# A graph attention layer on one core: narrower row levels in the first sort, and the second sort on keys without their offset taken off

## The chip, the cores and the metric

The kernel runs on one core of a Trainium2 chip. The metric is the device time of one execution in microseconds (us). In the profile lines TensorE is "PE" (its weight loads "PEld"), VectorE "DVE", ScalarE "ACT", GpSimd "POOL" and SyncE, which here only issues transfers, "SP"; L201 is a line of the kernel.

## The reference

```python
for h in range(n_heads):                       # 4 heads, 4096 nodes, 64 features
    x_proj[h] = x @ weight[h]
# a score for each of 50,000 edges (leaky relu of a source part plus a target part)
for h in range(n_heads):
    for i in range(num_edges):
        output[h, dst[i]] += np.exp(edge_scores[h, i]) * x_proj[h, src[i]]
# ... and each target's sum is divided by the sum of its exp(scores) + 1e-8
```

## The kernel before

Each of the 128 partitions holds 391 edges as fp32 keys in a row of 512; the rest of the row is padding with the largest key. A bitonic sort orders each row (levels k = 1 to 9) and then merges the rows of every 8 partitions into 16 runs. The key is ordered by the source's group (16 of them), then target, then source within the group. The runs go to DRAM, each group of 8 partitions fetches its own source group's windows back, a second sort merges them, and a second fetch gives windows by target. These are unpacked into indices for a loop over 33 blocks of 125 targets, which gathers with one-hot matmuls and sums with further matmuls.

A step of the sort is a minimum and a maximum over the first `width` columns:

```python
def half(self, j, width=L):
    s, d = self.step()                         # source and destination alternate
    h = 1 << j
    n = width >> (j + 1)
    for o, op in ((0, OP.min), (h, OP.max)):
        V.tensor_tensor(out=av(d[:], o, [2 * h, n], [1, h]), in0=av(s[:], 0, [2 * h, n], [1, h]),
                        in1=av(s[:], h, [2 * h, n], [1, h]), op=op)

def rows(self, first, n=L):
    w8 = -(-n // 8) * 8                        # 392 for the first sort, 512 for the second
    w128 = n // 128 * 128 if n % 128 <= 8 else L   # 384 and 512
    for k in range(first, 10):
        w = w8 if k <= 3 else w128 if k <= 7 else L
        self.flip(k, w)
        for j in range(k - 2, -1, -1):
            self.half(j, w)
        # ... (an assertion on which buffer is current)
```

The second sort takes the group's offset off the fetched keys first, and ScalarE counts how many keys lie below each of 33 bounds while VectorE sorts. The unpacking adds the block's offset from a per-partition column:

```python
def group(pool, pp, start):
    raw = pool.tile([P, L], F32, name="raw")
    fetch(pool, skey1, start, W1, raw, 1)
    kr = pool.tile([P, L], F32, name="kr")
    V.tensor_scalar(out=kr[:], in0=raw[:], scalar1=goff[:, 0:1], scalar2=None, op0=OP.add)
    sgn = below(pool, kr[:], L, nb2, ND, 8 * NI)     # 33 Sign activations with sums
    so = Sorter(pool, kr)
    so.rows(9)
    store(skey2, so.runs())
    bounds(pool, pp, sgn, 8 * NI, L, [sel2[:]], off2, m8, 8, ws2, we2)
# ...
# in unpack(i): kb = win[:, i] + boff[:, i], then a shift and a mask of kb, then a cast
```

## Time and profile before

| | before |
|---|---|
| median of the first runs | 305.47 us (304.89 to 305.67) |
| first sort's keys stored, at | 70.73 us |
| second sort's keys landed, at | 78.51 us |
| first unpacking, at | 122.43 us |
| first one-hot of the loop, at | 127.41 us |
| last result, at | 295.48 us |

Two lines of the page of the kernel before: busy time and share of the span by engine, and the clock granted to TensorE in 40 equal slices, in tenths of full speed:

```profile
PE 203.1 (67%) x3534; PEld 192.0 (64%) x3534; DVE 267.4 (89%) x494; ACT 179.7 (60%) x352; POOL 26.1 (9%) x71
...
PEclk9999965555555555798999999999999999999998
```

No engine is full over the span, yet there are stages in which one is. The table by stretch, in the prediction below, shows them.

### The profile page before, as it was taken

The numbers are of one execution on the slowest core, as the hardware profiler recorded it, in microseconds if no ns is written. First come the engines' busy times: TensorE is split into PE (matmuls) and PEld (weight loads), VectorE is DVE, ScalarE is ACT, GpSimd is POOL, SyncE is SP. The second block draws the span as 40 slices with busy tenths as digits, with TensorE's granted clock in tenths as the row PEclk, the third lists the DMA queues.
The fourth block names the chain that finished last, engine by engine and source line by source line (L and its number), as shares of the span: only waits on it lengthen the run. The fifth ranks groups of instructions, "written<-read, shape, count | busy, mean of one in ns | idle before, by whom it ended". The sixth has DMA issues, their size and how long they took to land. (4 is left out here: it accounts for less than half of the span.)

```text
span 301.8 us, 8411 instructions
## 1 busy us (share of the span) xinstructions
PE 203.1 (67%) x3534; PEld 192.0 (64%) x3534; DVE 267.4 (89%) x494; ACT 179.7 (60%) x352; POOL 26.1 (9%) x71
## 2 busy tenths in 40 slices
PE   0002999940000000849999999999999999999990
PEld 0001699930000000349999999999999999999980
DVE  3999999996599997699999999999999999999970
ACT  2951700050499920337877877787777877787750
POOL 7880000001100001500000000000000000000000
PEclk9999965555555555798999999999999999999998
DMA  3035000000100000397486568766785578755012
GB/s 106 0 66 93 0 2 0 0 0 36 36 0 0 0 0 35 104 384 291 150 287 226 190 251 297 251 198 232 277 289 202 211 252 301 259 205 195 17 38 58
DMA packets 13070, 41.80 MB, mean 138 GB/s; under 512 B 3088, under 2 KB 8272, under 8 KB 8928
## 3 DMA queue, kind: packets, MB, share of 16 engines
q1 hardware_dynamic: 10632, 38.97, 36.5%
q10 hardware_dynamic: 1688, 1.55, 2.2%
q0 software_dynamic: 704, 0.66, 1.0%
q8 instruction: 30, 0.49, 0.7%
q14 instruction: 16, 0.13, 0.1%
HBM read 36.13 MB, written 5.05 MB: 136 GB/s over the span
## 5 line engine op out<-in xcount | busy, mean ns | idle before, releaser
L464 ACT CAST xs<-ps 128x1200 bf16<-128x1200 f32 (+1 forms) x98 | 102.7, 1048 | 0.0
L477 DVE TENSOR_TENSOR val<-xs,wv 128x4096 bf16<-128x4096 bf16 (+1 forms) x34 | 75.7, 2229 | 4.6 <-ACT xs L464 1.0
L456 PE MATMUL ps<-xa,oh 128*128 128x72 bf16 x528 | 72.5, 197 | 3.6 <-DVE oh L438 2.9
L460 PE MATMUL ps<-adb,oh 128*128 128x136 bf16 x528 | 73.5, 226 | 0.0
L458 PE MATMUL ps<-xa,oh 128*128 128x72 bf16 x528 | 71.7, 198 | 0.6 <-DVE oh L439 0.5
L496 PE MATMUL acc<-xs,val 128*128 128x125 bf16 x1056 | 63.7, 218 | 1.2
L496 PEld LDWEIGHTS <-val 128*128 128x128 bf16 x1056 | 59.1, 98 | 3.5 <-DVE val L477 3.5
L456 PEld LDWEIGHTS <-oh 128*128 128x128 bf16 x528 | 52.4, 100 | 3.5 <-DVE oh L438 3.5
L458 PEld LDWEIGHTS <-oh 128*128 128x128 bf16 x528 | 52.1, 99 | 2.0 <-DVE oh L439 1.4
L460 PEld LDWEIGHTS <-oh 128*128 128x128 bf16 x528 | 52.2, 99 | 0.0
L462 ACT ACTIVATE ex<-ps 128x96 bf16<-128x96 f32 (+1 forms) x99 | 25.0, 253 | 30.1 <-PE ps L460 30.1
L438 DVE TENSOR_SCALAR oh<-bc,pF 128x4096 bf16<-128x4096 bf16 (+2 forms) x35 | 42.7, 1219 | 0.1
L201 DVE TENSOR_TENSOR sA<-sB 128x256 f32<-128x256 f32 (+2 forms) x108 | 39.6, 408 | 1.8
L201 DVE TENSOR_TENSOR sB<-sA 128x256 f32<-128x256 f32 (+2 forms) x100 | 36.8, 409 | 1.7
L263 ACT ACTIVATE junk<-kr,nb 128x512 f32<-128x512 f32 x33 | 23.8, 722 | 13.6 <-DVE kr L314 12.5
L274 PE MATMUL cnt_ps<-sgn,sel 128*128 128x17 f32 (+1 forms) x6 | 1.7, 390 | 43.9 <-ACT sgn L266 43.9
L274 PEld LDWEIGHTS cnt_ps<-sgn,sel 128*128 128x128 f32 x6 | 1.4, 318 | 44.0 <-issue 44.0
L358 PEld LDWEIGHTS at_ps<-uv,xT 64*128 64x128 f32 x130 | 25.4, 303 | 0.2 <-issue 0.2
L358 PE MATMUL at_ps<-uv,xT 64*128 64x4 f32 x130 | 25.5, 332 | 0.0
L439 DVE TENSOR_SCALAR oh<-bc,pF 128x2048 bf16<-128x2048 bf16 (+2 forms) x35 | 25.1, 717 | 0.0
L542 PE MATMUL pf<-Wbd,aT 128*125 128x128 f32 x132 | 21.9, 288 | 0.9 <-ACT aT L538 0.9
L341 PE MATMUL ps<-ident,wS 64*128 64x64 f32 x2 | 0.7, 350 | 27.7 <-DMA wS<-in_weight_dram 27.7
(126 smaller groups left out, 219.3 us busy)
## 6 DMA issues: line engine op xcount, KB each, us to landing
bc<-gat_bins SPq DMA_DIRECT2D x32, 1024.0 KB, 9.0
out_dram<-res SPq DMA_DIRECT2D x32, 125.0 KB
gat_sorted<-sA SPq DMA_DIRECT2D x2, 256.0 KB
eS<-in_edge_index_dram SPq DMA_DIRECT2D x1, 390.0 KB
eD<-in_edge_index_dram ACTq DMA_DIRECT2D x1, 390.0 KB
gat_bins<-tb SPq DMA_DIRECT2D x9, 32.0 KB
out_dram<-res SPq DMA_DIRECT2D x1, 96.0 KB
win<-gat_sorted,wi POOLq DMA_INDIRECT x5, 2.6
```

Source lines behind the costliest of these rows:

```text
L201: V.tensor_tensor(out=av(d[:], o, [2 * h, n], [1, h]), in0=av(s[:], 0, [2 * h, n], [1, h]), in1=av(s[:], h, [2 * h, n], [1, h]), op=op)
L263: S.activation(out=junk[:], in_=v, func=ACTF.Sign, bias=nbnd[:, b:b + 1], scale=1.0, accum_out=sgn[:, b:b + 1])
L358: T.matmul(out=ps[:, b, :], lhsT=xT[:, b * step:b * step + P], rhs=uv[:, k, :], start=(b == 0), stop=True, skip_group_check=True)
L438: V.tensor_scalar(out=oh[:, 0:2, e], in0=bc[:, :, e], scalar1=pF[:, 0:1], scalar2=None, op0=OP.is_equal)
L439: V.tensor_scalar(out=oh[:, 2, e], in0=bc[:, 1, e], scalar1=pF[:, 1:2], scalar2=None, op0=OP.is_equal)
L456: T.matmul(out=ps[:, i, P:P + XC], lhsT=oh[:, 1, e], rhs=xa[:, 2 * t, :], start=(i % 2 == 0), stop=False, skip_group_check=True)
L458: T.matmul(out=ps[:, i, P:P + XC], lhsT=oh[:, 2, e], rhs=xa[:, 2 * t + 1, :], start=False, stop=False, skip_group_check=True)
L460: T.matmul(out=ps[:, i, 0:S0], lhsT=oh[:, 0, e], rhs=adb[:, b, :], start=False, stop=True, skip_group_check=True)
L462: S.activation(out=av(ex[:], 2 * t0, [2, n], [2 * NT, 2 * H], [1, 2]), in_=av(ps[:], P, [PW, n], [1, 2 * H], [0, 2]), func=ACTF.Exp)
L464: copy(out=xs[:, t0:t0 + n, 0:P + XC], in_=ps[:, 0:n, 0:P + XC])
L477: V.tensor_tensor(out=av(val[:], h * Dout, [Dout, n], [C, NT], [1, Din]), in0=av(xs[:], S0, [0, n], [XW, NT], [1, Din]), in1=av(wv[:], h * ...
L496: T.matmul(out=self.acc[:, k * BD:(k + 1) * BD], lhsT=val[:, t, k * P:(k + 1) * P], rhs=xs[:, t, 0:BD], start=False, stop=(t == NT - 1), s ...
```

## The change

The intent is to take work off VectorE where it works alone. The steps of levels 8 and 9 skip columns that hold padding only. The second sort compares the keys as they were fetched, since all keys of a run share one offset and their order does not depend on it; ScalarE takes the offset off for its counts, and the unpacking's column carries it for the rest. GpSimd prepares that column in the setup.

```diff
     boff = cst.tile([P, NI], F32)
+    pg = cst.tile([P, 1], F32)
+    G.tensor_scalar(out=pg[:], in0=pm16[:], scalar1=-float(SG * N), scalar2=None, op0=OP.mult)
     for i in range(NI):
         G.tensor_scalar(out=boff[:, i:i + 1], in0=p16[:], ...)
+        G.tensor_tensor(out=boff[:, i:i + 1], in0=boff[:, i:i + 1], in1=pg[:], op=OP.add)
@@ rows
                 for j in range(k - 2, -1, -1):
-                    self.half(j, w)
+                    self.half(j, w if k <= 7 or j > 6 else w128 if j > 2 else w8)
@@ group
-        V.tensor_scalar(out=kr[:], in0=raw[:], scalar1=goff[:, 0:1], scalar2=None, op0=OP.add)
+        S.activation(out=kr[:], in_=raw[:], func=ACTF.Identity, bias=goff[:, 0:1])
         sgn = below(pool, kr[:], L, nb2, ND, 8 * NI)
-        so = Sorter(pool, kr)
+        so = Sorter(pool, raw)
```

## The prediction

> **What bounds the kernel now.** I first read the table of busy time by stretch, cutting the span where the timelines of the engines show a change of work. VectorE is "DVE", ScalarE "ACT", GpSimd "POOL", TensorE "PE".
>
> ```profile
> core 0: us, PE busy (x) PEld busy (x) DVE busy (x) ACT busy (x) POOL busy (x), PEclk, DMA share, GB/s
> 5.70:26.40 20.70, 0.00 (x0) 0.00 (x0) 19.60 (x61) 13.35 (x35) 14.89 (x34) 1.00 0.29 58
> 26.40:39.80 13.40, 10.79 (x63) 8.11 (x63) 12.86 (x34) 6.93 (x13) 0.00 (x0) 1.00 0.00 0
> 39.80:70.60 30.80, 23.70 (x112) 23.57 (x111) 29.46 (x74) 4.50 (x5) 0.00 (x0) 0.50 0.00 1
> ...
> 78.50:116.90 38.40, 0.62 (x2) 0.50 (x2) 36.74 (x92) 27.08 (x67) 0.00 (x0) 0.50 0.00 0
> ...
> 200.00:240.00 40.00, 39.68 (x846) 38.82 (x843) 38.69 (x41) 31.35 (x58) 0.00 (x0) 1.00 0.68 241
> ```
>
> The kernel is three stages in a row. From 5.7 to about 70.6 us VectorE alone runs the first sort; its tenth of idle time is the few hundredths between dependent instructions. From 78.5 to 116.9 it runs the second sort. After about 123 us a loop over 33 blocks keeps PE busy 39.68 of 40 us and DVE 38.69. The share for the whole span (DVE 89%, PE 67%) hides this: before 123 us only DVE's own chain counts, and both parts of the change lie there. The chain that ended last is no help, since it reaches back only to 284.8 us.
>
> Next, the timeline of VectorE in the first sort, where a row is start, length, engine, line, operation, output, input and count. The rows differ in their width only:
>
> ```profile
> 9.03 0.64 DVE L201 TENSOR_TENSOR sA<-sB 128x196 f32<-128x196 f32 x2
> 9.70 0.36 DVE L191 TENSOR_TENSOR sB<-sA 128x196 f32<-128x196 f32 x1
> ...
> 24.37 0.63 DVE L201 TENSOR_TENSOR sB<-sA 128x192 f32<-128x192 f32 x2
> 25.04 0.63 DVE L201 TENSOR_TENSOR sA<-sB 128x192 f32<-128x192 f32 x2
> ...
> 33.51 0.76 DVE L201 TENSOR_TENSOR sB<-sA 128x256 f32<-128x256 f32 x2
> 34.31 0.76 DVE L201 TENSOR_TENSOR sA<-sB 128x256 f32<-128x256 f32 x2
> ```
>
> A step (one min, one max) starts every 0.67 us at 196 columns a half, 0.66 at 192, and 0.795 at 256 (34.31 to 35.10 gives 0.79, eight steps in a row average 0.795). Start to start is what counts on a chain, not the length of one. The level k = 8 begins at 26.36 and is the first at full width.
>
> Last, the head and the end of the second sort, on VectorE and then on ScalarE:
>
> ```profile
> 78.51 0.49 DVE L314 TENSOR_SCALAR kr<-raw,goff 128x512 f32<-128x512 f32 x1 [5.08 <-DMA raw<-gat_sorted,wi]
> 79.03 0.43 DVE L191 TENSOR_TENSOR sA<-kr 128x256 f32<-128x256 f32 x1
> ...
> 116.94 0.19 DVE L276 TENSOR_SCALAR cnt<-cnt_ps 128x41 f32<-128x41 f32 x1
> ```
>
> ```profile
> 79.17 0.72 ACT L263 ACTIVATE junk<-kr,nb 128x512 f32<-128x512 f32 x1 [12.54 <-DVE kr L314]
> ...
> 107.11 0.20 ACT L266 COPY sgn<-sgn 128x7 f32<-128x7 f32 x1
> ```
>
> The fetched keys land, VectorE subtracts the group's offset (it waited 5.08 us for the transfer), and only then do the sort and ScalarE's 33 counts start. The counts end at 107.31, and their result is first wanted at 116.94.
>
> [...] I found one table load in the trace, 1.28 us at 5.68, in front of the first Sign[...]. [...] Here the six steps from 7.68 to 11.71, beside POOL's setup, took 4.03 us, 0.672 each, against 0.668 worked out from the quiet 192-column steps[...]; no loss to speak of.
>
> **The change part by part.**
>
> Row levels. In k = 8 the halves j = 6 to 3 go from 512 columns to 384 and j = 2 to 0 to 392; in k = 9 the same, while its j = 7 and both flips stay full. With 391 edges a row, columns 392 to 511 hold only the padding maximum, so the skipped comparisons change nothing. Steps per level: four at 384 and three at 392, two levels: 8 x (0.795 - 0.660) = 1.08 us and 6 x (0.795 - 0.668) = 0.76 us, together 1.84 us. All of it is on VectorE's chain. The second sort has 512 real columns, so its widths stay.
>
> Offset of the second sort. The subtraction leaves VectorE: 79.03 - 78.51 = 0.52 us from the chain, since the first flip now waits for the transfer itself. In its place ScalarE runs one Identity of 512 elements, about 0.72 us (what a Sign of this shape takes in the row above), ahead of the counts. Its first Sign came 0.66 us after the keys landed; now it comes after 0.72 us and a hand-over that I put at 0.17 (kr ended at 79.00, Sign began at 79.17), 0.23 us later. Counts then end 107.31 - 78.51 + 0.23 = 29.0 us after landing, and VectorE wants them 116.94 - 78.51 - 0.52 = 37.9 us after. About 0.6 us of matmul between leaves 8 us of slack. Nothing is lost there.
>
> Unpacking. The offset goes into boff, a per-partition column that the unpacking already adds. Those five VectorE instructions (about 0.29 us each) stay as they are.
>
> Setup on POOL. One more tensor_scalar and five tensor_tensor on one column. The existing five boff instructions took 1.64 us, 0.33 each, so six take about 2.0 us. POOL's later transfers go out 2 us later. Its att vectors are issued by 19.3 and land 2.2 us later, near 21.5; moved to 23.5 they still precede PE's use at 28.36, which comes after weights that land at 27.68. boff itself is used at 122.4. Hidden.
>
> Sum: 1.84 + 0.52 = 2.36 us off a chain that sets the start of the loop. The store, second fetch and loop follow by data, and loop blocks repeat at a fixed rhythm, so all of it should reach the end: 305.47 - 2.36 = 303.11 us. The before median lies high in what was seen (304.89 to 305.67, and 304.22 for the profiled execution), so I put **303.0**.
>
> **The rivals.** (1) *TensorE's clock eats or adds to the gain.* [...] The trace has such a half-clock stretch at the loop's start, 135.4 to 138.7 (0.50 in those windows, 1.00 just before). If that were lost time, it is worth half of 3.3, 1.65 us, at most[...]. For it: PE is nearly full from there on. Against: the runs before spread over only 0.8 us. Times 301.4 to 304.8, the ends unlikely. (2) *ScalarE's counts become the bound of the second sort*, gaining nothing from the 0.52 and leaving 303.6. The 8 us of slack speaks against. (3) *A wait moves in.* The store's landing and the indirect fetch could hide part of the gain, if they were tied to something else; but both fetches follow VectorE's last instructions (the store goes out at 70.73, right at the end of the sort), so they move along. [...] (4) *Narrow steps save less*, if the fixed part of an instruction were all that mattered: refuted by the 0.66 against 0.795 above.
>
> **Range and chances.** The mechanism is arithmetic on durations of the same instructions; what is unsure is the clock's phase (about 0.7 us as I weigh it) and the median of few runs (0.4). Together some 0.8 either way: 302.1 to 304.0. Two per cent would be 6.1 us, more than twice the whole sum, so faster by over 2% gets 0.01, slower 0.01, same 0.98.
>
> **What would show it.** In the changed trace the fourteen steps should read 0.66 or 0.67 us start to start and the first sort's store go out near 68.9 in place of 70.73. The first flip of the second sort should start as the transfer lands, with an Identity on ScalarE beside it, no table load, counts ending about 29 us after landing and the sort about 37.9 after. The first unpacking should start near 120.1 instead of 122.43, and the blocks of the loop keep their rhythm. I am wrong if a new wait stands before the first flip, if VectorE's steps beside POOL's setup slow down, or if the half-clock stretch grows or goes and the loop's length with it.

The 0.668 us of a step at 196 columns is an estimate from the two widths in the trace: 64 columns are 0.795 - 0.660 = 0.135 us a step, so 4 more than 192 are 0.008. That the Identity would bring no table load was the assumption. The clock's phase in the range means when the half-clock stretch comes; the 0.7 us for it is an estimate out of the 1.65, and that the stretch could come otherwise was not shown by then (c1 shows it later: 10.2 us in place of 3.4).

## More of the kernel before

Lines of the changed kernel are numbered three higher from the middle on, and an experiment's may be a few more.

## The result

The changed kernel is correct and takes 302.82 us (median of 4 runs, 302.28 to 303.03) against 305.18 us (4 runs, 304.57 to 305.67). The ratio is 0.9921, with a 95% interval of 0.9897 to 0.9945. A ratio is the mean time of one kernel's fast runs over the mean of the other's in the same rounds, so it is not quite the ratio of the medians. The medians differ by 2.36 us.

The table by stretch of the changed kernel, cut where the same work begins and ends (columns as in the prediction):

```profile
core 0: us, PE busy (x) PEld busy (x) DVE busy (x) ACT busy (x) POOL busy (x), PEclk, DMA share, GB/s
5.64:26.34 20.70, 0.00 (x0) 0.00 (x0) 19.60 (x60) 13.34 (x35) 16.48 (x40) 1.00 0.27 57
26.34:38.07 11.73, 8.14 (x37) 5.57 (x38) 11.13 (x36) 6.20 (x12) 0.00 (x0) 1.00 0.01 3
38.07:68.83 30.76, 26.13 (x137) 25.63 (x134) 29.46 (x74) 5.28 (x7) 0.00 (x0) 0.56 0.00 1
76.68:114.62 37.94, 0.62 (x2) 0.50 (x2) 36.32 (x91) 27.80 (x68) 0.00 (x0) 0.50 0.00 0
200.00:240.00 40.00, 39.69 (x833) 38.83 (x831) 38.69 (x42) 31.74 (x59) 0.00 (x0) 1.00 0.70 246
```

Levels 8 and 9 are the second row: 11.73 us, where they took 13.52 (26.36 to the shuffle at 39.88). The levels beside GpSimd's setup, the first row, are as long as before (20.70 us) although GpSimd works 1.6 us more in it (16.48 us in place of 14.89). The merging, 30.76 us, took 30.74. The second sort, from the landing of its keys to the use of the counts, takes 37.94 in place of 38.43. The loop's own rates are the same.

The timeline of VectorE in level 8 of the changed kernel; the row at 29.78 starts 0.66 us after the one before it and is followed by one at 30.45:

```profile
28.46 0.63 DVE L204 TENSOR_TENSOR sB<-sA 128x192 f32<-128x192 f32 x2
29.12 0.63 DVE L204 TENSOR_TENSOR sA<-sB 128x192 f32<-128x192 f32 x2
29.78 0.64 DVE L204 TENSOR_TENSOR sB<-sA 128x196 f32<-128x196 f32 x2
```

The head of the second sort, VectorE first, then ScalarE:

```profile
76.68 0.43 DVE L194 TENSOR_TENSOR sA<-raw 128x256 f32<-128x256 f32 x1 [5.06 <-DMA raw<-gat_sorted,wi]
...
114.62 0.20 DVE L279 TENSOR_SCALAR cnt<-cnt_ps 128x41 f32<-128x41 f32 x1
```

```profile
77.11 0.72 ACT L317 ACTIVATE kr<-raw,goff 128x512 f32<-128x512 f32 x1 [9.79 <-DMA raw<-gat_sorted,wi]
77.87 0.72 ACT L266 ACTIVATE junk<-kr,nb 128x512 f32<-128x512 f32 x1
```

The first comparison itself now waits for the transfer, and ScalarE's Identity and counts run beside the sort. The counts end at 106.0 us, far ahead of 114.62. No table load stands before the Identity: the only one in the trace is at 5.64 us (1.28 us), in front of the first Sign, as before.

The first unpacking on VectorE, in the kernel before and then in the changed one:

```profile
122.43 0.29 DVE L379 TENSOR_SCALAR kb<-win,boff 128x128 int32<-128x128 f32 x1 [2.02 <-DMA win<-gat_sorted,wi]
```

```profile
120.14 0.29 DVE L382 TENSOR_SCALAR kb<-win,boff 128x128 int32<-128x128 f32 x1 [2.04 <-DMA win<-gat_sorted,wi]
```

One thing moved that nobody asked to move. TensorE's first work, on the weights, in the changed kernel:

```profile
28.60 0.34 PE L344 MATMUL ps<-ident,wS 64*128 64x64 f32 x1 [28.60 <-DMA wS<-in_weight_dram]
```

It began at 27.68 before. The eight small transfers of the att vectors, issued 2 us later by GpSimd, landed 2.1 to 7.6 us after their issue, where they had taken 2.1 to 2.7. The tables ended at 63.2 us in place of 62.5, which VectorE did not feel, since it asks for the result at 68.83.

### The profile page after: what moved, and what is told of

Read it like the earlier page. It is cut to its first block, busy times and chain, and to the rows that moved or that the text cites. A ratio compares the mean times of both kernels' runs of the same rounds, so it can differ in the third digit from the quotient of the medians.

```text
span 300.1 us, 8417 instructions
## 1 busy us (share of the span) xinstructions
PE 203.3 (68%) x3534; PEld 191.8 (64%) x3534; DVE 265.2 (88%) x493; ACT 180.4 (60%) x353; POOL 27.6 (9%) x77
## 5 line engine op out<-in xcount | busy, mean ns | idle before, releaser
L204 DVE TENSOR_TENSOR sA<-sB 128x256 f32<-128x256 f32 (+2 forms) x108 | 38.8, 400 | 1.9
L204 DVE TENSOR_TENSOR sB<-sA 128x256 f32<-128x256 f32 (+2 forms) x100 | 35.9, 400 | 1.7
L361 PEld LDWEIGHTS at_ps<-uv,xT 64*128 64x128 f32 x130 | 24.7, 296 | 0.4 <-issue 0.4
L361 PE MATMUL at_ps<-uv,xT 64*128 64x4 f32 x130 | 24.8, 327 | 0.0
```

Source lines behind the costliest of these rows:

```text
L361: T.matmul(out=ps[:, b, :], lhsT=xT[:, b * step:b * step + P], rhs=uv[:, k, :], start=(b == 0), stop=True, skip_group_check=True)
```

## The experiments

Where each run stands at the same points of the program, in us of its profile; the times are medians of the kernel and of the kernel before on the same chip.

| run | store | keys landed | counts used | first unpacking | first one-hot | last result | time | before |
|---|---|---|---|---|---|---|---|---|
| before | 70.73 | 78.51 | 116.94 | 122.43 | 127.41 | 295.48 | 305.18 | |
| changed | 68.94 | 76.68 | 114.62 | 120.14 | 125.58 | 293.51 | 302.82 | 305.18 |
| a1_rows_only | 68.85 | 76.64 | 115.09 | 120.59 | 126.07 | 294.12 | 302.45 | 304.13 |
| a2_offset_only | 70.83 | 78.58 | 116.51 | 122.11 | 127.14 | 295.08 | 303.68 | 304.13 |
| a3_all_wide | 74.49 | 82.20 | 120.65 | 126.19 | 131.59 | 299.52 | 308.28 | 304.13 |
| a4_after_again | 68.98 | 76.66 | 114.60 | 120.15 | 124.98 | 293.15 | 301.86 | 304.13 |
| b1_counts_late8 | 68.92 | 77.03 | 114.91 | 120.46 | 125.85 | 294.43 | 302.95 | 304.50 |
| b2_counts_late24 | 68.84 | 76.86 | 124.66 | 128.95 | 135.66 | 304.32 | 312.43 | 304.50 |
| b3_pool_late40 | 68.93 | 78.61 | 116.49 | 122.02 | 126.91 | 295.06 | 303.34 | 304.50 |
| b4_clock_held | 68.86 | 76.58 | 114.46 | 119.99 | 124.90 | 292.29 | 301.46 | 304.50 |
| c1_after_ref | 68.92 | 76.72 | 114.66 | 120.20 | 125.13 | 294.41 | 302.08 | 304.71 |
| c2_warm_early | 69.12 | 76.80 | 114.72 | 120.25 | 125.16 | 293.64 | 302.37 | 304.71 |
| c3_both_clock | 69.10 | 76.63 | 114.56 | 120.10 | 124.97 | 293.00 | 301.58 | 304.71 |
| c4_unpack_spread | 68.94 | 76.69 | 114.62 | 120.17 | 124.63 | 294.83 | 303.22 | 304.71 |

All results were correct. The theory is that VectorE's chain sets when the loop starts and the rest follows. Its rivals are the clock of TensorE, the counts on ScalarE, and a wait that moves in.

**Each part alone.** a1 is the kernel before with this edit, and a2 the kernel before with all the other edits of the change:

```diff
-                    self.half(j, w)
+                    self.half(j, w if k <= 7 or j > 6 else w128 if j > 2 else w8)
```

> The kernel before with the narrow row levels alone. My theory (VectorE's chain sets the start of the loop): the first sort's store goes out near 68.9 us instead of 70.73, the first unpacking starts near 120.6 instead of 122.43, and the time falls by 1.84 us. Rival 1[...]: unpacking as above, but the end of the span moves by less or more than 1.84 by up to 1 us. Rival 3 (a wait hides it): the store moves, the unpacking does not.

> The kernel before with the offset's move alone. Theory: store unmoved near 70.7, the first unpacking near 121.9 (0.52 us earlier), the time 0.5 us lower, which lies near the noise of a run, so the trace decides. Rival 2 (ScalarE's counts bind): the unpacking stays at 122.4.

VectorE's timeline in a1, then in a2:

```profile
76.64 0.49 DVE L314 TENSOR_SCALAR kr<-raw,goff 128x512 f32<-128x512 f32 x1 [5.10 <-DMA raw<-gat_sorted,wi]
...
120.59 0.28 DVE L379 TENSOR_SCALAR kb<-win,boff 128x128 int32<-128x128 f32 x1 [2.02 <-DMA win<-gat_sorted,wi]
```

```profile
78.58 0.42 DVE L194 TENSOR_TENSOR sA<-raw 128x256 f32<-128x256 f32 x1 [5.06 <-DMA raw<-gat_sorted,wi]
...
122.11 0.29 DVE L382 TENSOR_SCALAR kb<-win,boff 128x128 int32<-128x128 f32 x1 [2.11 <-DMA win<-gat_sorted,wi]
```

In a1 the landing moves by 1.87 us and the unpacking by 1.84. In a2 nothing moves before the landing, and from the landing to the use of the counts it takes 116.51 - 78.58 = 37.93 us against 38.43: 0.50 us. The unpacking shows only 0.32 of it, since this execution was already 0.07 late at the landing and the window came another 0.11 later. By time, a1 is 0.995 (0.9928 to 0.9971) of before and a2 0.9989 (0.997 to 1.0008). The second interval holds 1: the total time cannot show half a microsecond, but the trace can. A wait that hides the gain is out.

**All levels wide.** The same lever the other way:

```diff
-            w8 = -(-n // 8) * 8
-            w128 = n // 128 * 128 if n % 128 <= 8 else L
+            w8 = w128 = L
```

> The kernel before with no row level narrowed at all: all 512 columns in levels 1 to 9. This is the same lever pushed the other way, to see the size per step and whether the end follows one to one. 22 steps go from 192 to 256 columns a half (0.135 us each) and 6 from 196 to 256 (0.127), flips among them 4 and 3, which makes 26 steps of the first kind and 6 of the second: 26 x 0.135 + 6 x 0.127 = 4.3 us. Theory: the store near 75.0, the unpacking near 126.7, the time 4.3 us above the kernel before. A rival in which the loop start is set by something else would move the end by clearly less than 4.3.

The expectation has a slip. The 22 steps already count the flips, so the sum is 22 x 0.135 + 6 x 0.127 = 3.73 us, not 4.3. The store, from SyncE's timeline:

```profile
74.49 0.35 SPq L254 DMA_DIRECT2D gat_sorted<-sA  x1
```

It came 3.76 us after that of the kernel before, the unpacking 3.76 and the last result 4.04. The size per step holds. By time a3 is 1.0141 (1.0119 to 1.0164) of before, 4.15 us by medians. The end follows with about 0.3 us more, which must come from between the unpacking and the end.

**The whole change again.**

> The changed kernel again, on the same chip and in the same rounds as its parts. If the parts are independent, its gain over the kernel before is the sum of those of a1 and a2, 2.36 us by my working, within 0.4. In the trace the store near 68.9 and the unpacking near 120.1, as before[...].

a4 is 0.9923 (0.9905 to 0.994) of before, 2.27 us by medians. The parts gave 1.68 and 0.45, together 2.13.

From the first one-hot to the last result, the kernel before, the changed kernel and a1 to a4 took 167.93 to 168.17 us. From the unpacking to the first one-hot they took 4.83 to 5.48. So the few tenths by which the end does not follow lie in front of the loop, where TensorE spreads the first window for ScalarE to copy. TensorE's granted clock goes with them. Where it rose to 1.00 within 2.9 us of the first unpacking (before 2.7, a2 2.9, a4 2.5), the first one-hot came 4.8 to 5.0 us after the unpacking; where it rose after 3.6 to 4.1 us (changed, a1, a3), it came after 5.4 to 5.5.

**ScalarE's counts later.** The changed kernel with 8 or 24 activations that nobody reads:

```diff
+        idle = pool.tile([P, L], F32, name="idle")
+        for _ in range(8):          # 24 in b2
+            S.activation(out=idle[:], in_=raw[:], func=ACTF.Identity, bias=goff[:, 0:1])
         S.activation(out=kr[:], in_=raw[:], func=ACTF.Identity, bias=goff[:, 0:1])
```

> The changed kernel with eight idle Identities on ScalarE ahead of the counts (correct result). In the changed trace the counts end at 106.0 us, their matmul at about 106.7, and VectorE asks for them at 114.62: 7.9 us of slack. Eight of 0.65 to 0.76 us take 5.2 to 6.1. Theory (slack, counts are off the path): unpacking stays near 120.1, time unchanged within 0.3 per cent. Rival 2 (the counts already bind or share something with VectorE): 5 us slower, or VectorE's steps longer than 0.795.

> The same with 24 idle Identities, 15.6 to 18.2 us. Theory: the slack of 7.9 us is used up, VectorE's bounds wait 7.7 to 10.3 us; some 0.7 us of that is won back since the store has landed by then. Unpacking near 127 to 130, the time 7 to 9.6 us longer. If it is 15 or more longer, there was no slack; if unchanged, ScalarE is not waited for here at all.

In b1 the eight took 6.0 us, and landing to use of the counts is 37.88 us, as in the changed kernel: the counts are off the path. Yet b1 came to 0.9955 of before (0.993 to 0.9981), more than expected. Its profile shows where: VectorE loses 0.3 us ahead of the first fetch's indices, and 0.35 us in each of two blocks of the loop. Each time it stands between two instructions, and what the profile names as the releaser had long been done. b2 lost 0.35 in the same two blocks. Something in these programs other than the counts costs about 1 us; what it is stays open. In b2, ScalarE first, then VectorE:

```profile
77.02 18.11 ACT L319 ACTIVATE idle<-raw,goff 128x512 f32<-128x512 f32 x24 [9.64 <-DMA raw<-gat_sorted,wi]
```

```profile
124.66 0.20 DVE L279 TENSOR_SCALAR cnt<-cnt_ps 128x41 f32<-128x41 f32 x1 [9.84 <-PE cnt_ps L277]
```

VectorE waits 9.84 us for 18.1 us of idle work: the slack is about 8 us, as worked out. The unpacking moved by 8.8, since its wait for the window was only 0.80 us in place of 2.04; that the store had landed by then is the likely reason, which no run tested. By time b2 is 1.0254 (1.0231 to 1.0278) of before, some 10 us above the changed kernel's 0.992 and more than the 7 to 9.6 expected. The profile has 1.3 us of that in front of the loop: from unpacking to first one-hot took 6.71 us in place of 5.44, and the clock rose only 5.0 us after the unpacking. So ScalarE would be the bound if its part grew by 8 us, and it grew by under 1.

**GpSimd's setup longer.** The changed kernel with 41 more one-column operations after the new ones:

```diff
+    pq = cst.tile([P, 1], F32)
+    G.tensor_copy(out=pq[:], in_=pg[:])
+    for _ in range(40):
+        G.tensor_tensor(out=pq[:], in0=pq[:], in1=pg[:], op=OP.add)
     m16 = cst.tile([P, 16], F32)
```

> The changed kernel with 41 more one-column operations in GpSimd's setup, at 0.30 to 0.335 us about 12 to 13.4 us. Theory: what was added by the change (2 us) is hidden because TensorE's tables have slack; pushed further, the att vectors are issued by 33 to 34.7 and land near 36 to 37, TensorE's tables start about 7.5 us later, its count matmuls end near 71.7 in place of 64.2, and VectorE, which wants them at 68.83, loses about 3 us there; the time rises by 2 to 4 us. VectorE's steps beside GpSimd's longer setup stay at 0.66 to 0.67 us[...].

GpSimd's timeline, then TensorE's, then VectorE's:

```profile
11.84 13.15 POOL L150 TENSOR_TENSOR pq<-pq,pg 128x1 f32<-128x1 f32 x40
```

```profile
25.36 0.34 PE L348 MATMUL ps<-ident,wS 64*128 64x64 f32 x1 [25.36 <-DMA wS<-in_weight_dram]
34.41 0.34 PE L352 MATMUL ps<-attbd,wT 128*64 128x4 f32 x2 [8.72 <-DMA attbd<-in_att_dst_dram]
```

```profile
70.92 0.18 DVE L283 TENSOR_SCALAR cnt<-cnt_ps 128x17 f32<-128x17 f32 x1 [2.02 <-PE cnt_ps L281]
```

The store stands at 68.93: 40 one-column operations at 0.33 us beside VectorE's steps cost VectorE nothing that shows. Beside GpSimd's three 128-column comparisons (tile `sel`) VectorE did lose a little. In the kernel before, the VectorE instructions at 11.71 and 12.42 us, each inside one of the last two of them, took 0.41 us in place of 0.36. In the changed kernel GpSimd reaches them 1.95 us later, and now those at 13.65 and 14.37 took 0.41. What slowed them was not shown; it is 0.1 us in both kernels, so the change neither pays nor saves it.

TensorE now waits 8.72 us for the att vectors, and VectorE 2.02 for TensorE; the landing moves by 1.93, the unpacking by 1.88. By time b3 is 0.9957 (0.9934 to 0.998) of before, about 1.1 us above the changed kernel's 0.992 where 2 to 4 were expected. The loss is smaller than the 3 us expected; that the weights landed at 25.36 in place of 28.60 may be a part of it. With the att vectors issued 13 us later, these landed 2.1 to 2.2 us after their issue again, and the weights came sooner. That agrees with the 0.9 us by which the change itself delayed them: TensorE began at 28.46 to 28.91 in the ten other profiles with the change's setup, and at 27.50 to 27.82 in the three without it (before, a1, a3). So the 2 us added to the setup are hidden; 15 are not.

**The clock held.** The changed kernel with 18 matmuls that nobody reads, in the gap between the first block's gather and the second's:

```diff
                 self.gather(0, c, V.tensor_copy if c == 1 else S.copy)
+            hold = self.psa.tile([P, AW], F32, name="acc")
+            for _ in range(18):
+                T.matmul(out=hold[:, 0:2 * BD], lhsT=identb[:], rhs=av(adb[:], 0, [1, 2 * BD]), start=True, stop=True)
```

> The changed kernel with 18 dense matmuls[...] in the gap of 2.5 us in which TensorE waits for the second block's one-hot, so that the half-clock stretch of 3.4 us at the loop's start, seen in all six profiles so far, should not come. My prediction put its worth at 1.65 us at most. View A (the stretch is lost time): the loop, 168.0 us from the first one-hot to the last result in six profiles, shrinks by up to 1.65 us. View B (VectorE sets the pace at the start, the stretch lies in its shade): below 0.3 us.

By estimate from the loop's matmuls of 125 columns, 32 of which took 1.76 us at the full clock in the kernel before (206.43 to 208.19), 18 of 250 columns take about 2.0 us of the gap's 2.5.

Stretches of 2 us at the loop's start (the column after POOL is the granted clock): the changed kernel, the changed kernel in run c1, and b4.

```profile
132.00:134.00 2.00, 1.10 (x25) 0.99 (x26) 1.90 (x4) 0.00 (x0) 0.00 (x0) 1.00 0.99 295
134.00:136.00 2.00, 2.00 (x39) 2.00 (x37) 2.00 (x2) 1.42 (x3) 0.00 (x0) 0.51 1.03 336
136.00:138.00 2.00, 2.00 (x29) 2.00 (x28) 1.58 (x3) 2.00 (x4) 0.00 (x0) 0.64 1.05 328
```

```profile
132.00:134.00 2.00, 1.47 (x18) 1.33 (x19) 1.90 (x4) 0.00 (x0) 0.00 (x0) 0.50 0.94 340
134.00:136.00 2.00, 2.00 (x40) 2.00 (x39) 2.00 (x2) 1.30 (x2) 0.00 (x0) 0.50 1.09 336
136.00:138.00 2.00, 2.00 (x25) 2.00 (x23) 1.34 (x3) 1.81 (x4) 0.00 (x0) 0.50 1.06 397
```

```profile
132.00:134.00 2.00, 1.57 (x44) 1.58 (x45) 1.90 (x3) 0.65 (x2) 0.00 (x0) 1.00 0.80 248
134.00:136.00 2.00, 1.80 (x40) 1.68 (x37) 2.00 (x2) 2.00 (x5) 0.00 (x0) 1.00 1.03 383
136.00:138.00 2.00, 2.00 (x42) 2.00 (x40) 1.90 (x4) 1.18 (x3) 0.00 (x0) 1.00 0.99 393
```

In the changed kernel's profile the half clock lasts some 3.4 us and follows the gap. In c1, an execution of the same kernel, it lasts about 10 and begins at 128.8, before the gap of 130.1 to 132.1. In b4 it does not come. The first two periods of the loop (start to start of the weighting on VectorE) are 4.77 + 5.49 = 10.26 us, 5.41 + 6.08 = 11.49 and 4.39 + 5.34 = 9.73. So b4 is 0.53 us faster there than the changed kernel's profile, and 0.53 to 0.77 than the six profiles with the short stretch; c1 is 1.76 slower than b4. Only the first of these is what the 18 matmuls can have won: c1's stretch began before the place where they stand. The later periods alternate between 5.28 and 4.42 in all three. One-hot to last result is 167.39 us in b4, and b4 is 0.9898 of before (0.988 to 0.9916). View B is out. Of the 1.65 us that view A allowed at most, about 0.6 came; the rest of the stretch lies beside VectorE's work.

**Towards a better version.** c1 is the changed kernel again, as the reference on this chip.

> The changed kernel once more as the reference for the next three on this chip: 0.992 of the kernel before, as twice so far (0.9921 and 0.9923).

It is 0.9917 of before (0.9898 to 0.9935). c2 moves the warming matmuls, nine whose result nobody reads, and c3 adds b4's edit to it:

```diff
         longest(so2, pp2, ws1, we1, 0)
+        warm = pp2.tile([P, L], F32, name="warm")
+        for i in range(3):
+            T.matmul(out=warm[:], lhsT=identb[:], rhs=adb[:, 0:4, 0:P], start=True, stop=True)
         longest(so2, pp2, ws2, we2, 1)
-        n1, n2 = room(0, EL), room(1, L)
-        warm = pp2.tile([P, L], F32, name="warm")
-        for i in range(9):
+        for i in range(6):
             T.matmul(out=warm[:], lhsT=identb[:], rhs=adb[:, 0:4, 0:P], start=True, stop=True)
+        n1, n2 = room(0, EL), room(1, L)
```

> The changed kernel with its nine warming matmuls moved: three between the two transposes of the longest windows and six right after, instead of nine after the counts are read back. In the changed profile the unpacked bins are ready at 121.18, but TensorE is busy warming until 122.5, and the spread then ran at half clock until 123.9. From the first unpacking to the first one-hot the seven profiles that are alike here took 4.8 to 5.5 us. Theory: the spread now starts about 1.3 us earlier and mostly at full clock, but VectorE still has the unpackings 1 to 3 to do until about 125.0, so the first one-hot comes at most 0.56 us earlier than in the changed profile; 0.1 to 0.6 us of time. Rival: the clock does not rise in time and nothing is gained.

> c2 and the held clock of b4 together. If they are independent: loop 167.4 us as in b4, first one-hot as in c2, so 0.6 to 1.2 us under the changed kernel.

c2 gained nothing: 0.9927 (0.9909 to 0.9945), and the first one-hot at 125.16 is where other executions of the changed kernel have it (124.98, 125.13). Its premise did not come about. TensorE stood idle from 120.15 to 122.28, so the spread began 0.25 us earlier than the 122.53 of the changed profile and not 1.3, and the clock fell to a half at 122.6. What the spread waited for is open.

c3 is 0.9901 (0.9881 to 0.992), its first two periods 9.73 us again, but the two edits are not independent. Its loop took 168.03 us in place of the 167.4 expected: from the first one-hot to the first weighting it took 8.34 us, and 7.71 in b4, with the clock at a half from 122.7 to 129.5. By time it is b4's gain with nothing added.

c4 is c3 with the unpackings 2 and 3 moved into the loop, and 4, which was in the loop already, moved to a later block (the expectation counts it among those ahead of the loop):

```diff
-        for i in range(1, 4):
-            win.unpack(i, nc.sync, nc.sync)
+        win.unpack(1, nc.sync, nc.sync)
         blocks.spread(0, win.tb[:, 0])
-        blocks.run({i - 3: lambda i=i: win.unpack(i, nc.sync, nc.sync) for i in range(4, NI)})
+        blocks.run({4 * i - 5: lambda i=i: win.unpack(i, nc.sync, nc.sync) for i in range(2, NI)})
```

> c3 with the unpackings 2 to 4 put into the loop after the blocks 3, 7 and 11, in place of three of them ahead of the first one-hot. View A (the loop has slack on VectorE: 38.7 of 40 us busy): up to 1.5 us is gained over c3, as the first one-hot no longer waits for two unpackings of 1.0 us. View B (VectorE and TensorE are co-bound, so what leaves the start comes back as longer periods of three blocks, 5.28 or 4.42 us each before): no gain over c3 within 0.3 us, and the loop's length grows by about what the start wins.

VectorE in the loop, at the same place in c3 and then in c4:

```profile
151.74 0.75 DVE L442 TENSOR_SCALAR oh<-bc,pF 128x2048 bf16<-128x2048 bf16 x1
152.41 0.22 DVE L475 TENSOR_TENSOR wv<-ex 128x128 bf16<-128x128 bf16 x1
```

```profile
150.81 0.75 DVE L442 TENSOR_SCALAR oh<-bc,pF 128x2048 bf16<-128x2048 bf16 x1
151.48 0.28 DVE L382 TENSOR_SCALAR kb<-win,boff 128x128 int32<-128x128 f32 x1
...
152.40 0.22 DVE L475 TENSOR_TENSOR wv<-ex 128x128 bf16<-128x128 bf16 x1
```

The unpacking begins the moment the one-hot is done and pushes the next instruction back by 152.40 - 151.48 = 0.92 us. The three periods that now hold an unpacking are 5.34 us where they were 4.42, and the second, which held unpacking 4 in c3, is 4.77 where it was 5.34: the loop grew by 2.17 us (168.03 to 170.20). The start won only 0.34 us (124.97 to 124.63), since VectorE then stood 1.92 us in front of the first one-hot. c4 is 0.9957 of before (0.9939 to 0.9974), 1.6 us worse than c3 by medians. View A is out. View B is right that nothing is gained, but not in size: the loop grew by far more than the start won. VectorE has no slack in the loop, although its busy time reads 38.69 of 40 us and TensorE's 39.69.

Two things in the changed kernel's profile say the same. Between 200 and 240 us it has no wait of VectorE for another engine, while ScalarE waits 7.8 us in all for TensorE. And the periods alternate between 5.28 and 4.42 us because every other one also holds VectorE's division of two blocks by their sums (0.89 us, from 205.85 to 206.74).

The version with the least time is b4, the changed kernel with its clock held: 301.46 us against 304.50 for before. Against the changed kernel the intervals overlap (0.988 to 0.9916 and 0.9905 to 0.994 from different calls; c3 against c1 on one chip is 301.58 to 302.08 us), so the gain of some half microsecond rests on the trace more than on the time.

## Why the prediction was right

The prediction was 303.0 us; measured were 302.82, and 2.36 us between the medians, the very sum. That it is the very sum is luck: the same pair differs by 2.27 us in a4's call and by 2.63 in c1's.

- *VectorE alone counts before the loop*: shown by a1, a2 and a3, in which store, landing and unpacking move by the amount taken from or given to its chain. A slip on the way: the idle share of VectorE in the first sort is a twentieth (19.60 of 20.70 us busy, 29.46 of 30.80), not a tenth, which is the share over the whole span; nothing rests on it.
- *Row levels, 1.84 us*: levels 8 and 9 took 1.79 us less (13.52 to 11.73). The fourteen steps start 0.66 to 0.67 us apart. The error is 0.05.
- *Offset, 0.52 us*: 0.50 in a2, 0.49 in the changed kernel.
- *Hand-over on ScalarE, 0.23 us later*: mis-sized. The first Sign came 77.87 - 76.68 = 1.19 us after the landing in place of 0.66, so 0.53 later, since ScalarE began its Identity 0.43 us after VectorE began on the same landed keys. It did so in all nine profiles with the plain Identity, but 0.16 us after in b1 and b2, where an idle one comes first; why is open. The delay is hidden in 8 us of slack, which b2 measured.
- *Setup hidden*: right in effect. The mechanism had a gap: I took the att vectors' landing time as fixed at 2.2 us. Issued 2 us later, the last of them fell beside the weights' transfer, which is issued from 19.5 on; their landing time rose to as much as 7.6, and the weights came 0.9 us later. b3 shows where a later setup begins to count. The six steps taken as proof of no loss beside GpSimd stop at 11.71, just short of the two slower ones.
- *All of it reaches the end*: right within the noise of the clock. In the profiled pair the unpacking moved by 2.29 us, the first one-hot by 1.83, the last result by 1.97. The missing tenths go with rival 1: the clock rose 2.7 us after the unpacking before, and 3.6 in the changed profile, and the first one-hot then came 0.46 us later after the unpacking. No run held the clock there with success (c2 tried), so this is read from the traces and not tested.
- *Rival 1, at most 1.65 us, some 0.7 as weighed*: about right in size. Two executions of the same kernel differ by 1.23 us in the first two periods, and b4, without the stretch, is 0.53 and 1.76 below them. The most was a little more than 1.65 because the stretch lasted three times as long in c1 as the one seen (10.2 us against 3.3). The prediction looked for it at the loop's start only; in front of the loop it counts too. Its grounds had a wrong piece: it leaned on TensorE being nearly full in the loop, and c4 shows that VectorE sets the loop's pace.
- *Rivals 2, 3 and 4*: 2 fell in b1 (landing to use of the counts unchanged). 3 fell in a1 to a3, where landing and unpacking follow the store, and in b3 VectorE's steps were unchanged beside 40 more one-column operations of GpSimd. 4 fell with the fourteen steps.

## What to carry to other kernels

In a chain of dependent instructions on one engine, price a change by start to start of the same instructions at the two widths, and check that the stages after it follow by data alone; here the sum (2.36 us) then reached the end (2.36 us between the medians). Test slack by filling it with idle work until the wait appears, which gives its size as well as its existence (8 us here, in b2). A busy share does not say which engine paces a loop (here TensorE's read 39.69 of 40 us and VectorE's 38.69, and VectorE set the pace): put one more microsecond on an engine and see whether the period grows, and look whether the engine waits for any other.

## What the traces show of the chip in this case

- TensorE's clock and a gap: in the kernel before TensorE stood idle for 2.5 us (131.8 to 134.3), having been busy only 0.93 and 1.59 of the two 2 us stretches before it, and its granted clock was 0.50 from 135.4 to 138.7. The half clock followed the gap in ten of the eleven profiles without the added matmuls, and in none of the three with them (b4, c3, c4). In c1 it came at 128.8 us without any such gap: TensorE was busy 1.79 of the 3.4 us before, and not idle for more than 1.0 us at a time. These stretches lasted 3.4 us in the changed kernel's profile, 6.8 in c3 (ahead of the loop) and 10.2 in c1; what sets their length, and what started the one in c1, was not shown.
- Dependent instructions on VectorE: one fp32 tensor_tensor of 256 columns took 0.42 to 0.43 us. A minimum and its maximum, which do not need each other, start 0.34 us apart (26.34 and 26.68); the next step, which needs both, starts 0.46 later (27.14).
- ScalarE after VectorE on one and the same landed transfer: it started 0.43 us later (77.11 against 76.68), and 0.16 later in b1 and b2.
